# A hybrid decoder layer on one core: the last layer norm without GpSimd arithmetic, its bias written ahead and added to by transfers

## The chip, the core and the metric

The kernel runs on one core of a Trainium2 chip. A core has a matrix engine (TensorE, in the profile PE, its weight loads PEld), three engines for elementwise work (VectorE = DVE, ScalarE = ACT, GpSimd = POOL), an engine that here only issues transfers (SyncE = SP), and 16 DMA engines that move data between the memory of the chip (DRAM) and the core's own memory (SBUF). Matrix products land in PSUM, eight banks of 128 x 512 f32. The metric is the time of one execution in microseconds on the device: the median over several runs.

## The reference, cut to what matters

One decoder layer on 1024 tokens of 1024 channels: a token mixer (convolution, state-space model, attention), a first layer norm, and a mixture of experts with a shared expert, then a second layer norm. All is f32. The change is in the second norm and its inputs:

```
y = routed_experts(h2d, e_idx, e_w, ...) + swiglu(h2d, shared ...)
x = layer_norm(DEEPNORM_ALPHA * x + g2 * y, ln_g[l, 1], ln_b[l, 1])

def layer_norm(x, g, b):            # over the 1024 channels of a token
    mu = mean(x); var = mean(square(x - mu))
    return (x - mu) * rsqrt(var + 1e-5) * g + b
```

Each token goes to two experts, so the routed part of y is a sum of two rows.

## The kernel before, in words

The stages stand in `build` one after the other: `mixer` (with `front`, the state-space parameters on POOL, and the projections), `attention`, `merge` (output weights of the attention branch, gates), `ffn` (first norm, routing, shared expert), `experts` (blocks of 128 rows, one after the other, inside conditional stretches), `final`.

`experts` writes each result row, already weighted, by an indirect transfer on POOL's queue (line 1672) into a DRAM array `yd` of 2 x 1024 rows: first choices, then second choices. The shared expert's part and the residual are already summed in eight SBUF tiles `base[i]`, 128 tokens x 1024 channels each.

`final` works through the same eight tiles of 128 tokens. First it loads the gate g2, the gain and the bias of the norm as three rows of 4 KB on SP (line 1714), spreads each over 128 partitions by TensorE products with a row of ones (line 1719), and ACT copies the result to SBUF (line 1720). Sixteen loads of 512 KB on SP bring both rows of each token (line 1729); they wait for the last indirect transfer of the experts. Then, for a tile:

- `gated`: the two rows are added and multiplied by g2. For tiles 0 and 1 (`DG`) DVE does both on 128 x 1024 (lines 1735 and 1736). For the others TensorE adds them, with the identity as the weights (line 1741), and DVE multiplies out of PSUM in two halves (line 1742).
- `total`: DVE adds `base` and sums over channels in one instruction (line 1746), ACT makes the negative mean (1751) and the sum of squares (1753).
- `root`, `norm`: ACT makes variance and root (1759, 1760), DVE refines the reciprocal by three instructions on 128 x 1 (1763 to 1765).
- For tiles 0 to 4, ACT applies mean and scale (1775), and `affine` lets POOL multiply by the gain and add the bias (1781, two instructions on 128 x 1024). For tiles 5 to 7 (`LAST = 5`) DVE does it in two instructions (1798, 1783).
- SP stores the tile (line 1784).

Outside the stretches marked `manual_schedule` (parts of the front, the router and the experts), a planner orders the instructions of every engine before the kernel runs. It takes them by their place in the program, but one that has nothing to wait for can be put ahead of earlier ones that have. On the chip each engine and each of its queues goes through its instructions in that order.

Of the kernel before, what the change touches and what calls it, by code (L numbers as in the profile page):

```python
# [10 lines left out]
F32 = mybir.dt.float32  # L11
# [3 lines left out]
AF = mybir.ActivationFunctionType  # L15
ALU = mybir.AluOpType
# [4 lines left out]
D = 1024  # L21
S = 1024
NT = S // 128
# [20 lines left out]
LN_EPS = 1e-5  # L44
# [23 lines left out]
LT = 5  # L68
LGI, DV, DG = 2, (6, 7), (0, 1)
# [11 lines left out]
class K:  # L81
# [86 lines left out]
    def build(self):  # L168
        with ExitStack() as ctx:
# [24 lines left out]
                self.attention()  # L194
            if self.stop == "att":
                return
            self.mgp = pool(est, "mgp")
            self.mh, self.ml = ([self.part(z, c) for c in range(4)] for z in "hl")
            self.wof = pool(est, "wof")
# [1506 lines left out]
    def final(self, P):  # L1706

        nc = self.nc
        v, act, gp, pe = nc.vector, nc.scalar, nc.gpsimd, nc.tensor
        ys = []  # L1710

        row = P.tile([128, 3, D], F32, name="frow")
        for i, src in enumerate((self.adad[3:4, :], self.a["ln_g"][1:2, :], self.a["ln_b"][1:2, :])):
            nc.sync.dma_start(out=row[0:1, i], in_=src)
        g2, lg, lb = (P.tile([128, D], F32, name=n) for n in ("g2", "lg2", "lb2"))
        for i, t in enumerate((g2, lg, lb)):
            for n in range(2):
                ps, sl = self.ps("y"), slice(n * 512, (n + 1) * 512)
                pe.matmul(ps[:], self.ones[0:1, :], row[0:1, i, sl], start=True, stop=True)
                act.copy(out=t[:, sl], in_=ps[:])  # L1720
        st = P.tile([128, 6, NT], F32, name="fst")
        eps = P.tile([128, 1], F32, name="feps")
        v.memset(eps[:], LN_EPS)

        act.activation(out=st[:, 5, 0:1], in_=self.ones[:, 0:1], func=AF.Sqrt)
        for i in range(NT):
            ys.append([P.tile([128, D], F32, name=f"fy{k}", tag=f"fy{k}", bufs=NT) for k in range(2)])
            for k in range(2):
                nc.sync.dma_start(out=ys[i][k][:], in_=self.yd[k * S + i * 128:k * S + (i + 1) * 128, :])
        c = lambda n, i: st[:, n, i:i + 1]  # L1730

        def gated(i, n):
            if i in DG:
                if n == 0:
                    v.tensor_tensor(out=ys[i][0][:], in0=ys[i][0][:], in1=ys[i][1][:], op=ALU.add)
                    v.tensor_tensor(out=ys[i][0][:], in0=ys[i][0][:], in1=g2[:], op=ALU.mult)
                return
            sl = slice(n * 512, (n + 1) * 512)
            ps = self.ps("y")
            for k in range(2):  # L1740
                pe.matmul(ps[:], self.ident[:], ys[i][k][:, sl], start=k == 0, stop=k == 1)
            v.tensor_tensor(out=ys[i][0][:, sl], in0=ps[:], in1=g2[:, sl], op=ALU.mult)

        def total(i):
            r = ys[i][0]
            v.scalar_tensor_tensor(out=r[:], in0=r[:], scalar=1.0, in1=self.base[i][:], op0=ALU.mult, op1=ALU.add,
                                   accum_out=c(0, i))
            if i in DV:
                v.tensor_scalar(out=c(2, i), in0=c(0, i), scalar1=-1.0 / D, scalar2=None, op0=ALU.mult)
            else:  # L1750
                act.mul(out=c(2, i), in_=c(0, i), mul=-1.0 / D)
            junk = P.tile([128, D], BF, name="junk", tag="junk", bufs=2)
            act.activation(out=junk[:], in_=r[:], func=AF.Square, bias=c(2, i), accum_out=c(3, i))

        def root(i):
            if i in DV:
                v.tensor_scalar(out=c(3, i), in0=c(3, i), scalar1=1.0 / D, scalar2=LN_EPS, op0=ALU.mult, op1=ALU.add)
            else:
                act.activation(out=c(3, i), in_=c(3, i), func=AF.Identity, scale=1.0 / D, bias=eps[:])
            act.activation(out=c(4, i), in_=c(3, i), func=AF.Sqrt)  # L1760

        def norm(i):
            v.reciprocal(out=c(4, i), in_=c(4, i))
            v.scalar_tensor_tensor(out=c(5, i), in0=c(4, i), scalar=c(3, i), in1=c(4, i), op0=ALU.mult, op1=ALU.mult)
            v.tensor_scalar(out=c(5, i), in0=c(5, i), scalar1=-0.5, scalar2=1.5, op0=ALU.mult, op1=ALU.add)
            if i in DV:
                v.tensor_tensor(out=c(4, i), in0=c(4, i), in1=c(5, i), op=ALU.mult)
            else:
                act.activation(out=c(4, i), in_=c(4, i), func=AF.Identity, scale=c(5, i))
            if i < LAST:  # L1770
                if i in DV:
                    v.tensor_tensor(out=c(2, i), in0=c(2, i), in1=c(4, i), op=ALU.mult)
                else:
                    act.activation(out=c(2, i), in_=c(2, i), func=AF.Identity, scale=c(4, i))
                act.activation(out=ys[i][0][:], in_=ys[i][0][:], func=AF.Identity, scale=c(4, i), bias=c(2, i))

        def affine(i):
            r = ys[i][0]
            if i < LAST:
                for e, row, op in zip(GL[i], (lg, lb), (ALU.mult, ALU.add)):  # L1780
                    (v if e == "v" else gp).tensor_tensor(out=r[:], in0=r[:], in1=row[:], op=op)
            else:
                v.scalar_tensor_tensor(out=r[:], in0=ys[i][1][:], scalar=c(4, i), in1=lb[:], op0=ALU.mult, op1=ALU.add)
            nc.sync.dma_start(out=self.out[i * 128:(i + 1) * 128, :], in_=r[:])

        GL = ('gg', 'gg', 'gg', 'gg', 'gg', 'vv', 'vv', 'vv')
        LAST = LT
        with ExitStack():
            for j in range(NT + 2):
                if j < NT:  # L1790
                    gated(j, 0)
                    gated(j, 1)
                if 0 < j < NT:
                    root(j - 1)
                if j < NT:
                    total(j)
                    if j >= LAST:
                        v.scalar_tensor_tensor(out=ys[j][1][:], in0=ys[j][0][:], scalar=c(2, j), in1=lg[:], op0=ALU.add, op1=ALU.mult)
                    if j == NT - 1:
                        norm(j - 1)  # L1800
                        affine(j - 1)
                        affine(j - 2)
                        root(j)
                        norm(j)
                        affine(j)
                        break
                if j:
                    norm(j - 1)
                if j > 1:
                    affine(j - 2)  # L1810


class Route:
# [290 lines left out]
```

## Time and profile before

| | us |
|---|---|
| median of 3 runs | 1587.35 (1585.13 to 1588.13) |
| the profiled execution, its own time | 1582.0 |
| its span | 1579.9 |
| PE busy | 1419.6 (90%) |
| DVE busy | 1196.8 (76%) |
| ACT busy | 733.4 (46%) |
| POOL busy | 442.5 (28%) |

The span runs from the first to the last record of the profile; the execution's own time is 2.1 us longer. Mean granted TensorE clock: 0.954 of full speed. Times in the rows below are microseconds from the span's start unless they are marked ns.

### The profile page before, as it was taken

What the parts mean: (1) busy time and instruction counts of PE and PEld (TensorE: products, weight loads), DVE (VectorE), ACT (ScalarE), POOL (GpSimd) and SP (SyncE); (2) the same over time, 40 slices, a digit from 0 to 9 for tenths busy, and PEclk for the clock granted to TensorE, in tenths of its full rate; (3) what the DMA queues carried; (4) which work ended last, traced back from release to release, by engine and by line L of the source; (5) the groups of instructions that cost most, each with busy time, mean ns of one, the idle gap of its engine ahead of it and who ended that gap; (6) DMA issues with size and microseconds to landing.
All of it is one profiled execution on the core that took longest, in us unless ns stands there. A gap on an engine that the chain in (4) does not pass through costs nothing.

```text
span 1579.9 us, 20183 instructions
## 1 busy us (share of the span) xinstructions
PE 1419.6 (90%) x6996; PEld 1144.4 (72%) x6996; DVE 1196.8 (76%) x1861; ACT 733.4 (46%) x1192; POOL 442.5 (28%) x599
## 2 busy tenths in 40 slices
PE   5599799479999999999799979999979999999983
PEld 3477678368888887887588867788967888888841
DVE  8464687898775547756587788778887999999948
ACT  6232112242223334130477763335424998999853
POOL 7999930000000000006211252400322322222216
PEclk9799999799999999999799998999999999999977
DMA  9232221132122248968200035634623777777643
GB/s 382 80 113 88 73 58 27 67 101 97 56 107 107 107 145 308 326 161 224 36 15 12 4 114 192 225 133 151 251 79 115 303 282 287 289 297 272 255 182 146
DMA packets 79940, 247.50 MB, mean 157 GB/s; under 512 B 18460, under 2 KB 29780, under 8 KB 71000
## 3 DMA queue, kind: packets, MB, share of 16 engines
q1 hardware_dynamic: 53670, 200.47, 36.0%
q10 hardware_dynamic: 15218, 24.68, 4.5%
q0 software_dynamic: 10944, 20.99, 4.2%
q8 instruction: 56, 0.92, 0.2%
q14 instruction: 52, 0.43, 0.1%
HBM read 252.74 MB, written 55.10 MB: 195 GB/s over the span
## 4 chain that ended last, share of the span: by engine, by line
PE 58%; DVE 14%; POOL 12%; DMA 7%; issue 5%; ACT 3%; ACTq 0%; DVEq 0%; POOLq 0%; SPq 0%
PE ps_mm L140 9%; PE ps_mm L141 9%; PE ps_mm L142 9%; DMA yd<-y,idx 4%; PE ps_up L140 3%; PE ps_h L140 3%; PE ps_h L142 3%; PE ps_h L141 3%; PE ps_up L141 3%; PE ps_up L142 3%; PE ps_O L1272 2%; PE ps_T L1258 2%; PE ps_y L140 1%; PE ps_y L142 1%; PE ps_tr L1635 1%
## 5 line engine op out<-in xcount | busy, mean ns | idle before, releaser
L1138 POOL TENSOR_TENSOR mg<-mg,sg 128x512 f32<-128x512 f32 x16 | 23.5, 1476 | 496.4 <-DVE sg L1137 492.8
L140 PE MATMUL ps_mm<-hh,wlo 128*128 128x512 f32 x304 | 123.5, 406 | 22.7 <-ACT sg L1075 15.6
L142 PE MATMUL ps_mm<-hh,whi 128*128 128x512 f32 x304 | 123.1, 405 | 0.0
L141 PE MATMUL ps_mm<-hl,whi 128*128 128x512 f32 x304 | 122.7, 404 | 0.0
L125 ACT CAST whi<-raw 128x1024 fp32r<-128x1024 f32 (+1 forms) x45 | 46.8, 1040 | 134.0 <-PE ps_up L142 65.2
L1672 POOL DMA_INDIRECT yd<-y,idx x33 | 46.5, 1409 | 170.4 <-ACT y L1671 98.4
L140 PEld LDWEIGHTS ps_mm<-hh,wlo 128*128 128x128 f32 x304 | 58.7, 193 | 37.6 <-ACT sg L1075 16.1
L129 DVE TENSOR_TENSOR qh<-wo,qh 128x1024 fp32r<-128x1024 f32 x66 | 80.5, 1220 | 5.1 <-ACT qh L125 5.1
L129 DVE TENSOR_TENSOR ql<-wo,ql 128x1024 fp32r<-128x1024 f32 x66 | 79.5, 1219 | 4.8 <-ACT ql L125 4.8
L129 DVE TENSOR_TENSOR wlo<-raw,whi 128x1024 fp32r<-128x1024 f32 x44 | 60.4, 1373 | 26.5 <-ACT whi L125 26.5
L125 ACT CAST qh<-wo 128x1024 fp32r<-128x1024 f32 x66 | 70.0, 1061 | 4.1 <-DMA wo<-exp 4.1
L142 PEld LDWEIGHTS ps_mm<-hh,whi 128*128 128x128 f32 x304 | 58.6, 193 | 14.9 <-issue 1.0
L141 PEld LDWEIGHTS ps_mm<-hl,whi 128*128 128x128 f32 x304 | 58.8, 193 | 13.7 <-issue 0.2
L125 ACT CAST ql<-wo 128x1024 fp32r<-128x1024 f32 x66 | 68.2, 1052 | 0.0
L125 ACT CAST xh<-ps_tr 128x512 fp32r<-128x512 f32 x66 | 39.5, 599 | 55.5 <-PE ps_tr L1635 55.4
L1610 POOL DMA_INDIRECT xg<-h2d,idx x35 | 37.1, 1061 | 77.1 <-PE ps_tr L1635 63.5
L1244 DVE TENSOR_REDUCE sm<-ps_S 128x1 f32<-128x256 f32 (+3 forms) x64 | 49.2, 770 | 10.8 <-PE ps_S L1241 10.1
L129 DVE TENSOR_TENSOR pl<-ps_T,ph 128x512 fp32r<-128x512 f32 (+1 forms) x80 | 45.9, 581 | 14.0 <-ACT ph L125 12.6
L140 PE MATMUL ps_up<-ah,wlo 128*128 128x512 f32 x128 | 50.6, 403 | 5.1 <-ACT ah L125 2.9
L391 DVE TENSOR_TENSOR sp<-ps_mm,sp 128x512 f32<-128x512 f32 x48 | 32.8, 686 | 28.0 <-PE ps_mm L142 27.8
L1245 ACT ACTIVATE p<-ps_S,sm 128x256 f32<-128x256 f32 (+3 forms) x64 | 48.5, 758 | 10.0 <-DVE sm L1244 9.4
L140 PE MATMUL ps_mm<-wo,ml 128*128 128x512 f32 x128 | 50.0, 398 | 2.8 <-DVE sg L1354 2.8
(727 smaller groups left out, 4733.2 us busy)
## 6 DMA issues: line engine op xcount, KB each, us to landing
wo<-exp SPq DMA_DIRECT2D x111, 1024.0 KB
raw<-w_in SPq DMA_DIRECT2D x43, 512.0 KB
adr<-w_ada SPq DMA_DIRECT2D x32, 512.0 KB
wada<-w_ada SPq DMA_DIRECT2D x16, 512.0 KB
fy<-yd SPq DMA_DIRECT2D x16, 512.0 KB
sga<-sg ACTq DMA_DIRECT2D x8, 512.0 KB
sgc<-sg ACTq DMA_DIRECT2D x8, 512.0 KB
sgs<-sg ACTq DMA_DIRECT2D x8, 512.0 KB
```

The lines of the kernel that those rows point to most:

```text
L125: nc.scalar.copy(out=hi, in_=src)
L129: e.tensor_tensor(out=lo, in0=src, in1=hi.bitcast(F32), op=ALU.subtract)
L140: mm(ps, wl, xh, start=first, stop=False)
L141: mm(ps, wh, xl, start=False, stop=False)
L142: mm(ps, wh, xh, start=False, stop=last)
L391: v.tensor_tensor(out=out, in0=p, in1=x, op=op)
L1244: v.tensor_reduce(out=sm[:], in_=x, axis=AX.XY if two else AX.X, op=ALU.max, negate=True)
L1245: act.activation(out=y, in_=x, func=AF.Exp, bias=sm[:], accum_out=d)
L1258: pe.transpose(pt[:, k2 * 256 + qi * 128:k2 * 256 + qi * 128 + 128], prob[h, c, qi][:, ks], self.ident[:])
L1272: pe.matmul(po[:, 0:256], vv[:, kt, h].rearrange("p z d -> p (z d)"), x[z], start=kt == 0 and z == 0, stop=kt == 2 * c + 1 and z == 1)
L1610: self.nc.gpsimd.indirect_dma_start(out=self.xg[b % 2][:], out_offset=None, in_=self.h2d[:], in_offset=bass.IndirectOffsetOnAxis(ap=self.i ...
L1672: nc.gpsimd.indirect_dma_start(out=self.yd[:], in_=y[:], in_offset=None, out_offset=bass.IndirectOffsetOnAxis(ap=self.idx[:, 1, b:b + 1], ...
```

## The change

In `build`, right behind the attention and ahead of the merge, SP gets one more transfer: the bias row is written to all 1024 rows of the output (4 MB, DRAM to DRAM). In `final`, the bias is gone from the arithmetic: every tile is finished in SBUF without it, and POOL issues a transfer that adds the tile to what stands in the output. TensorE adds the experts' rows of all eight tiles. POOL computes nothing. The gate and the gain come spread over 128 partitions by two transfers on ACT's queue; the rows, the products with ones and the copies are gone. All tiles have one form and one order.

```diff
@@ build, behind self.attention()
+            self.nc.sync.dma_start(out=self.out[:, :], in_=self.a["ln_b"][1:2, :].partition_broadcast(S))
@@ final
-        row = P.tile([128, 3, D], F32, name="frow")
-        for i, src in enumerate((self.adad[3:4, :], self.a["ln_g"][1:2, :], self.a["ln_b"][1:2, :])):
-            nc.sync.dma_start(out=row[0:1, i], in_=src)
-        g2, lg, lb = (...)            # each: 2 x (pe.matmul(ones, row) -> PSUM, act.copy -> SBUF)
+        g2, lg = (P.tile([128, D], F32, name=n) for n in ("g2", "lg2"))
+        nc.scalar.dma_start(out=g2[:], in_=self.adad[3:4, :].partition_broadcast(128))
+        nc.scalar.dma_start(out=lg[:], in_=self.a["ln_g"][1:2, :].partition_broadcast(128))
...
         def total(i):
             r = ys[i][0]
+            for n in range(2):
+                sl = slice(n * 512, (n + 1) * 512)
+                ps = self.ps("y")
+                for k in range(2):
+                    pe.matmul(ps[:], self.ident[:], ys[i][k][:, sl], start=k == 0, stop=k == 1)
+                v.tensor_tensor(out=r[:, sl], in0=ps[:], in1=g2[:, sl], op=ALU.mult)
             v.scalar_tensor_tensor(out=r[:], in0=r[:], scalar=1.0, in1=self.base[i][:], ..., accum_out=c(0, i))
+            act.mul(out=c(2, i), in_=c(0, i), mul=-1.0 / D)
             act.activation(out=junk[:], in_=r[:], func=AF.Square, bias=c(2, i), accum_out=c(3, i))
+            act.activation(out=c(3, i), in_=c(3, i), func=AF.Identity, scale=1.0 / D, bias=eps[:])
             act.activation(out=c(4, i), in_=c(3, i), func=AF.Sqrt)

         def norm(i):
+            q = ys[i][1]
+            v.scalar_tensor_tensor(out=q[:], in0=ys[i][0][:], scalar=c(2, i), in1=lg[:], op0=ALU.add, op1=ALU.mult)
             v.reciprocal(out=c(4, i), in_=c(4, i))
             ...                       # the same two 128 x 1 instructions on DVE
+            act.activation(out=c(4, i), in_=c(4, i), func=AF.Identity, scale=c(5, i))
+            act.activation(out=q[:], in_=q[:], func=AF.Identity, scale=c(4, i))
+            gp.dma_start(out=self.out[i * 128:(i + 1) * 128, :], in_=q[:], accum_op=ALU.add)
+
+        for i in range(NT + 1):
+            if i < NT:
+                total(i)
+            if i:
+                norm(i - 1)
```

`gated`, `root`, `affine` with its POOL instructions, the stores on SP, and the loop with its special cases for the last tiles are removed.

## Rows read from the trace of the kernel before

**Rows 1.** Chain of waits, its end: start us, length us, what.
```profile
1522.44 4.39 DMA fy<-yd
...
1526.93 1.23 DVE fy L1735
...
1574.62 1.28 DVE fy L1783
```

**Rows 2.** DVE groups, 1522 to 1580: line engine operation tiles shapes xcount | busy us, mean ns | idle.
```profile
L1746 DVE SCALAR_TENSOR_TENSOR fy<-fy,b 128x1024 f32<-128x1024 f32 x8 | 13.6, 1700 | 0.2
L1764 DVE SCALAR_TENSOR_TENSOR fst<-fst 128x1 f32<-128x1 f32 x8 | 9.7, 1208 | 0.1
L1742 DVE TENSOR_TENSOR fy<-ps_y,g 128x512 f32<-128x512 f32 x12 | 7.9, 682 | 0.0
L1798 DVE SCALAR_TENSOR_TENSOR fy<-fy,fst,lg 128x1024 f32<-128x1024 f32 x3 | 4.8, 1603 | 0.0
...
L1765 DVE TENSOR_SCALAR fst<-fst 128x1 f32<-128x1 f32 x8 | 1.2, 150 | 0.2
```

**Rows 3.** Timeline of the last norm, DVE and POOL: start, length, instruction [idle before <-releaser].
```profile
1529.52 1.23 DVE L1746 SCALAR_TENSOR_TENSOR fy<-fy,b 128x1024 f32<-128x1024 f32 x1
...
1536.81 0.22 DVE L1764 SCALAR_TENSOR_TENSOR fst<-fst 128x1 f32<-128x1 f32 x1
...
1537.84 5.67 POOL L1781 TENSOR_TENSOR fy<-fy,lg 128x1024 f32<-128x1024 f32 x2 [20.15 <-DVE fy L1742]
...
1538.56 2.72 DVE L1746 SCALAR_TENSOR_TENSOR fy<-fy,b 128x1024 f32<-128x1024 f32 x1
```

**Rows 4.** Timeline of the last norm, TensorE.
```profile
1520.42 10.57 PE L1719 MATMUL ps_y<-frow,ones 1*128 1x512 f32 x12 [4.71 <-DMA frow<-adad]
...
1531.85 23.11 PE L1741 MATMUL ps_y<-fy,ident 128*128 128x512 f32 x48 [0.86 <-DMA fy<-yd]
```

**Rows 5.** Windows: stretch, PE PEld DVE ACT POOL busy, granted clock, DMA share, GB/s.
```profile
80.00:84.00 4.00, 4.00 (x14) 3.15 (x13) 1.52 (x2) 1.39 (x2) 4.00 (x16) 0.71 0.00 0
...
1536.00:1538.00 2.00, 2.00 (x5) 0.83 (x4) 1.32 (x5) 1.97 (x7) 0.16 (x1) 0.90 1.02 406
...
1542.00:1544.00 2.00, 2.00 (x6) 0.88 (x5) 1.10 (x3) 1.30 (x4) 2.00 (x2) 1.00 0.97 387
```

**Rows 6.** ACT groups, 1515 to 1580.
```profile
L1753 ACT ACTIVATE junk<-fy,fst 128x1024 bf16<-128x1024 f32 x8 | 9.2, 1148 | 5.5 <-DVE fst L1749 5.3
L1775 ACT ACTIVATE fy<-fy,fst 128x1024 f32<-128x1024 f32 x5 | 6.2, 1241 | 0.1
L1769 ACT ACTIVATE fst<-fst 128x1 f32<-128x1 f32 x6 | 1.7, 287 | 3.5 <-DVE fst L1765 3.5
```

**Rows 7.** The mixer's 512 KB stores on POOL's queue: issue min/median/max ns; time to landing.
```profile
L1140 POOL DMA_DIRECT2D mgd<-mg x8: 556/568/797, 723.9 to 754.8; - x8
...
DMA to landing us min/median/max: 3.7/7.2/13.1
```

**Rows 8.** Windows of half a microsecond at the end of the span.
```profile
1577.50:1578.00 0.50, 0.00 (x0) 0.00 (x0) 0.00 (x0) 0.00 (x0) 0.00 (x0) 0.50 0.99 410
1578.00:1578.50 0.50, 0.00 (x0) 0.00 (x0) 0.00 (x0) 0.00 (x0) 0.00 (x0) 0.50 0.06 17
```

**Rows 9.** Timelines of the front: SP, ACT, PE.
```profile
19.39 2.85 SPq L118 DMA_DIRECT2D raw<-w_in  x3
...
75.75 0.78 ACT L579 ACTIVATE ht<-ps_x,col 128x512 f32<-128x512 f32 x1 [24.47 <-DMA csd<-sn]
...
76.58 1.12 PE L570 MATMUL ps_x<-ident,x 128*128 128x128 f32 x4 [18.20 <-ACT ht L579]
```

**Rows 10.** Attention: a window with a spread row, an idle one; ACT at its end.
```profile
868.00:869.00 1.00, 0.92 (x8) 0.91 (x8) 0.66 (x3) 0.93 (x4) 0.00 (x0) 1.00 1.04 254
...
885.00:895.00 10.00, 9.96 (x67) 8.30 (x66) 7.86 (x15) 7.77 (x21) 0.00 (x0) 1.00 0.00 0
...
937.84 1.05 ACT L125 CAST whi<-raw 128x1024 fp32r<-128x1024 f32 x1 [2.37 <-DMA raw<-w_up_attn]
```

More of the change, by code (lines that the diff above doesn't have):

```diff
@@ L1709, in final @@
         v, act, gp, pe = nc.vector, nc.scalar, nc.gpsimd, nc.tensor
-        ys = []
-        row = P.tile([128, 3, D], F32, name="frow")
-        for i, src in enumerate((self.adad[3:4, :], self.a["ln_g"][1:2, :], self.a["ln_b"][1:2, :])):
-            nc.sync.dma_start(out=row[0:1, i], in_=src)
[L1715 to L1720, printed above, removed]
+        g2, lg = (P.tile([128, D], F32, name=n) for n in ("g2", "lg2"))
+        nc.scalar.dma_start(out=g2[:], in_=self.adad[3:4, :].partition_broadcast(128))
+        nc.scalar.dma_start(out=lg[:], in_=self.a["ln_g"][1:2, :].partition_broadcast(128))
         st = P.tile([128, 6, NT], F32, name="fst")
@@ L1725, in final @@
         act.activation(out=st[:, 5, 0:1], in_=self.ones[:, 0:1], func=AF.Sqrt)
+        ys = [[P.tile([128, D], F32, name=f"fy{k}", tag=f"fy{k}", bufs=NT) for k in range(2)] for i in range(NT)]
         for i in range(NT):
-            ys.append([P.tile([128, D], F32, name=f"fy{k}", tag=f"fy{k}", bufs=NT) for k in range(2)])
             for k in range(2):
@@ L1730, in final @@
         c = lambda n, i: st[:, n, i:i + 1]
[L1732 to L1742, printed above, removed]
         def total(i):
             r = ys[i][0]
+            for n in range(2):
[4 more added lines that the diff above has]
+                v.tensor_tensor(out=r[:, sl], in0=ps[:], in1=g2[:, sl], op=ALU.mult)
             v.scalar_tensor_tensor(out=r[:], in0=r[:], scalar=1.0, in1=self.base[i][:], op0=ALU.mult, op1=ALU.add,
                                    accum_out=c(0, i))
[L1748 to L1751, printed above, removed]
+            act.mul(out=c(2, i), in_=c(0, i), mul=-1.0 / D)
             junk = P.tile([128, D], BF, name="junk", tag="junk", bufs=2)
             act.activation(out=junk[:], in_=r[:], func=AF.Square, bias=c(2, i), accum_out=c(3, i))
[L1755 to L1759, printed above, removed]
+            act.activation(out=c(3, i), in_=c(3, i), func=AF.Identity, scale=1.0 / D, bias=eps[:])
             act.activation(out=c(4, i), in_=c(3, i), func=AF.Sqrt)
         def norm(i):
+            q = ys[i][1]
+            v.scalar_tensor_tensor(out=q[:], in0=ys[i][0][:], scalar=c(2, i), in1=lg[:], op0=ALU.add, op1=ALU.mult)
             v.reciprocal(out=c(4, i), in_=c(4, i))
@@ L1765, in norm @@
             v.tensor_scalar(out=c(5, i), in0=c(5, i), scalar1=-0.5, scalar2=1.5, op0=ALU.mult, op1=ALU.add)
[L1766 to L1810, printed above, removed]
+            act.activation(out=c(4, i), in_=c(4, i), func=AF.Identity, scale=c(5, i))
```

## The prediction, made before the changed kernel ran

> **What bounds the kernel now.** Read the chain of waits from its end: it names the stage where time can be won. Its last 57 us are the last norm. The first pair of row loads lands at 1526.8 (1522.44 + 4.39), and from 1526.93 to 1574.62 + 1.28 = 1575.9 DVE is on the chain nearly without a break [rows 1]. So DVE bounds this stage: 49.0 us for eight tiles.
>
> Then the groups of DVE, to see what it does in that time. The sum over the tile (L1746) has a mean of 1700 ns and the smallest of instructions, 128 x 1 (L1764), a mean of 1208 ns [rows 2]. The timeline says why: alone, the same two take 1.23 and 0.22 us; the sum that starts at 1538.56 takes 2.72 us while POOL multiplies two SBUF tiles from 1537.84 on [rows 3]. DVE instructions with two SBUF operands are held up by POOL's. Against 1.21, 0.22 and 1.28 us undisturbed, the three lines lose 13.6 - 8 x 1.21 = 3.9, 9.7 - 8 x 0.22 = 7.9 and 4.8 - 3 x 1.28 = 1.0 us [rows 2, 3]: 12.8 us that are no work of DVE's.
>
> After DVE's end the last store goes. The windows show its data moving at 410 GB/s until shortly after 1578.0 [rows 8]; the span ends at 1579.9. The tail behind the last instruction is 4.0 us.
>
> TensorE works at half clock when the stage begins: twelve products of one row fill 1520.4 to 1531.0 [rows 4], the full ones start at 1531.85, and the granted clock is 0.90 in 1536 to 1538 and then 1.00 [rows 5]: full at about 1536.3, 4.4 us after their start. The front has another such rise: work begins at 76.58 after a pause of 18.2 us [rows 9], and 80 to 84 has a mean of 0.71 [rows 5], so the rise is near 82.3, 5.8 us after.
>
> **The change, part by part.**
>
> *POOL's arithmetic goes.* The 12.8 us of hold-ups go with it. DVE's own work in a tile becomes: two halves out of PSUM 2 x 0.68, sum with its readout 1.24, (x - mean) x gain 1.28 (L1798 undisturbed), three small instructions 0.53 together: 4.41 us, of which 2.60 in `total` and 1.81 in `norm` [rows 2, 3]. Eight tiles: 35.3 us against 49.0.
>
> *TensorE adds all rows.* It loses the cover that DVE's sums of tiles 0 and 1 gave it while the clock was low. A tile is 8 instructions. In the 23.11 us of its 48 [rows 4], 4.4 at half clock, one takes 20.9 / 48 = 0.435 us at 2.4 GHz and 0.87 at 1.2. It can start with the first 512 KB block, at about 1525.7 (half a pair earlier; the pairs follow at (1544 - 1526.9) / 7 = 2.4 us, the loads being over in the window 1542 to 1544 [rows 1, 5]). The two ACT-queue loads of gate and gain move 1 MB ahead of and beside the first blocks; they can be issued as the experts end, when the old rows were loaded, some 1.5 us ahead of the first product's 1520.42 [rows 4], and the row loads begin at 1522.44, so I charge 0.4 us of the 2.6 us that 1 MB takes at 400 GB/s; ends 0 and 2.6 [rows 1, 5]. Start 1526.1, half clock for 5.2 us (between the two rises): 6 instructions, so tile 0 is summed at 1531.3 + 2 x 0.435 = 1532.2, tile 1 at 1535.7, then one each 3.5 us, the last at 1556.6. The clock costs nothing more, since from tile 2 on 3.5 us are less than DVE's 4.41.
>
> *DVE.* Total of tile 0 is over at 1532.2 + 0.68 + 1.24 = 1534.1, of tile 1 at 1537.6. Should the planner put norm 0 into the gap ahead of tile 1, up to 1.3 us are won; I take the order of the program. Left are eight norms (14.5) and six totals (15.6): DVE ends at 1567.7, the last total at 1564.1.
>
> *ACT.* Per tile 1.15 + 0.19 for the squares, 1.24 for the scaling and four small ones of 0.2 to 0.29 [rows 6]: 3.6 us, under DVE's 4.41. At the end it becomes late: root of tile 7 at 1564.1 + 2.1 = 1566.2, scale of tile 6 until 1567.75, then tile 7's factor (0.29) and scaling (1.24): 1569.3. That is the new last instruction, 6.6 us ahead of the old.
>
> *The transfer that adds.* The trace has none. It has POOL's 512 KB stores, each taking the queue 0.57 us and landing 3.7 us (shortest), 7.2 (median), 13.1 (longest) after issue [rows 7]; nothing else of POOL's waits behind it now. What lies in the output has to be read too, 512 KB more: 1.3 us at 410 GB/s [rows 8]. Bounds for the tail: 4.0 us, as SP's store has now (the same bytes and one read more exclude a shorter one), and 0.3 + 13.1 + 1.3 + 0.9 = 15.6 by the longest landing. I take 0.3 wait + 3.7 + 1.3 + 0.9 from landing to the end of the span (of the 4.0 now I count 3.1 as issue and landing) = 6.2, because nothing else uses the DMA engines then: 2.2 more than now. The seven before it go beside DVE's work.
>
> The Trainium skill, "Collectives: The Full Stack", section on the bandwidth ceiling, says that a reducing transfer is slower by its two source reads and not by the addition, at half a copy's rate. By it one transfer would hold the engines for 2.6 us and eight for 21 us, spread over the 28 us from tile 0's end to the last: no queue, and the same tail. No run shown here has such a transfer.
>
> *The bias into the output.* 4.2 MB DRAM to DRAM have no row. At the 410 GB/s of the last store that is 10 us [rows 8]; at the 254 GB/s of a window in which one row is spread over many and the engines are full, 17 [rows 10]. It waits for nothing, so the planner may move it ahead of the attention, as it moved loads of `w_in` into the front's SP queue at 19.39, ahead of transfers that come earlier in the program [rows 9]. Inside the attention the DMA engines are idle (share 0.00 in 885 to 895) [rows 10]: price 0. In the front it delays the loads behind it, but there PE later idles 18.2 us and ACT 24.5 us, waiting for POOL's parameters [rows 9]: 10 to 17 us fit, price 0; above 18 the excess would count. I take 0; the bad place is a rival.
>
> *Removed rows, products, copies, bias instructions:* off the path or inside the DVE sum.
>
> **Sum.** Last instruction -6.6, tail +2.2: -4.4 us. The profiled execution's own time, 1582.0 (2.1 us around its span of 1579.9), becomes 1577.6; that execution lies 0.34% under the median of the runs shown, and scaled to the median 1587.35 it is 1582.9 us.
>
> **The rivals.**
>
> *The adding transfers become the bound.* Place: POOL's queue from about 1541.3 (tile 0 scaled). Eight at X us each end at 1541.3 + 8X + 4; that exceeds the old 1579.9 from X = 4.3 on. For it: the median landing of 7.2 and the longest of 13.1 [rows 7]. Against it: those shared the engines with loads, and a landing time is not an occupancy. At X = 5.5 it ends at 1589.3, 9.4 us later than before: 1597 us. Chance 0.12.
>
> *The bias goes right ahead of the merge's weights*, at its place in the program. At 937.84 ACT has already waited 2.37 us for the first of them [rows 10]; ACT and DVE stand still with the rest of the attention queued behind. 10 to 17 us come on the path, less 4.4: 1593 to 1600. Against it: the planner moves what is free to go. Chance 0.09.
>
> *The tail eats the gain.* The last transfer lands after the median of 7.2 plus the second read: tail 9.7, which is 5.7 more than now and 6.6 earlier: gain 0.9; or the clock rises 2 us later and the loads of gate and gain cost 2.6. Within 3 us of before: 1585.5. Chance 0.22.
>
> *Something elsewhere is re-ordered*, since a new SP instruction shifts the planner's times: slower by 4 to 8 us, chance 0.05.
>
> *It does not do what it says:* the bias may run in the front and not in the attention; by the above without a price, inside the forecast.
>
> **How the numbers follow.** The forecast has 0.52; its own range is 1579 (norm 0 in the gap, tail 4.0) to 1584. About 0.2%, 3.2 us, is what a measurement of this kernel can tell. Faster by more: 0.52, the forecast's. Same: 0.22, the tail. Slower: 0.12 + 0.09 + 0.05 = 0.26. The range 1578.5 to 1595 takes in the longest tail (15.6: 5.0 slower than before, 1592); it leaves out a few hundredths below, and above it half or more of the two slow rivals.
>
> **What would show it.** DVE's L1746 and L1764 successors at 1.2 and 0.22 us in all eight tiles; no POOL arithmetic after 1520; TensorE's sums starting near 1526 at half clock, full by 1532; DVE gapless from tile 2; last ACT scaling 6 to 7 us earlier than the old last DVE instruction; 6 us from there to the end. It is wrong if the adding transfers stand back to back after the last scaling, if DVE keeps waiting for PSUM after tile 2, or if the difference is already there before the experts begin.

## The result, and the profile after

| | before | after |
|---|---|---|
| median of 7 runs each, us | 1585.5 (1582.2 to 1588.1) | 1594.1 (1588.4 to 1600.8) |
| profiled execution, own time | 1582.0 | 1593.1 |
| its span | 1579.9 | 1591.0 |
| last indirect store of the experts issued (L1672, after L1674) | 1516.7 | 1529.1 |
| from there to the end of the span | 63.2 | 61.9 |

The change makes the kernel slower: ratio 1.0053, 95% interval 1.0033 to 1.0074, some 8.6 us. Forecast were 1582.9 us, 0.52 for faster. The last two rows of the table say where to look: the last norm is 1.3 us shorter, and everything ahead of it 12.4 us longer. The difference is there before the experts begin, which the prediction named as a sign of its being wrong.

The last norm first. DVE's groups in 1530 to 1591 of the kernel after (line numbers are 2 higher than before up to the last norm, whose lines are new):

```profile
L1734 DVE TENSOR_TENSOR fy<-ps_y,g 128x512 f32<-128x512 f32 x16 | 10.6, 680 | 11.8 <-PE ps_y L1733 11.8
L1745 DVE SCALAR_TENSOR_TENSOR fy<-fy,fst,lg 128x1024 f32<-128x1024 f32 x8 | 10.2, 1274 | 0.3 <-ACT fst L1737 0.3
L1735 DVE SCALAR_TENSOR_TENSOR fy<-fy,b 128x1024 f32<-128x1024 f32 x8 | 9.7, 1219 | 0.1
L1747 DVE SCALAR_TENSOR_TENSOR fst<-fst 128x1 f32<-128x1 f32 x8 | 1.7, 213 | 0.0
```

This is as forecast: against [rows 2], the sum has a mean of 1219 ns in place of 1700, and the smallest instruction 213 in place of 1208. POOL's hold-ups are gone, and once TensorE delivers (11.8 us idle) DVE has hardly a pause. TensorE starts 9.4 us after the experts' last indirect store, as forecast (1526.1 - 1516.7), at half clock, and is at full clock some 3.5 us later (0.54 in 1541 to 1542, 1.00 in 1542 to 1543). Its timeline, and then windows (the granted clock is the third column from the end; [rows 4, 5] are the old ones):

```profile
1538.44 22.14 PE L1733 MATMUL ps_y<-fy,ident 128*128 128x512 f32 x47 [10.39 <-DMA fy<-yd]
```

```profile
1538.00:1542.00 4.00, 3.56 (x5) 1.54 (x6) 0.00 (x0) 0.00 (x0) 0.00 (x0) 0.51 0.96 335
...
1574.00:1578.00 4.00, 0.00 (x0) 0.00 (x0) 0.72 (x5) 3.97 (x8) 1.72 (x2) 0.50 0.90 136
1578.00:1582.00 4.00, 0.00 (x0) 0.00 (x0) 0.00 (x0) 0.12 (x1) 0.86 (x1) 0.50 1.02 186
1582.00:1586.00 4.00, 0.00 (x0) 0.00 (x0) 0.00 (x0) 0.00 (x0) 0.00 (x0) 0.50 0.92 181
1586.00:1591.00 5.00, 0.00 (x0) 0.00 (x0) 0.00 (x0) 0.00 (x0) 0.00 (x0) 0.50 0.01 1
```

Read the end here: no engine computes after 1578.1, but the DMA engines (share in the last column but one) are full until about 1586 at 181 to 186 GB/s, where the old last store moved its data at 410 [rows 8]; then 5 us pass in which nothing moves. The last adding transfer is issued at 1578.4, 12.6 us ahead of the end; the old last store was 4.0 us ahead.

Now the write of the bias. One row of SP's queue, and three windows:

```profile
24.10 0.67 SPq L198 DMA_DIRECT2D out<-ln_b  x1
```

```profile
36.00:40.00 4.00, 3.99 (x20) 2.93 (x19) 1.95 (x4) 2.50 (x3) 3.65 (x7) 0.92 0.97 175
40.00:44.00 4.00, 3.27 (x15) 2.31 (x13) 0.00 (x0) 0.00 (x0) 3.71 (x7) 1.00 0.98 210
44.00:48.00 4.00, 0.00 (x0) 0.00 (x0) 0.00 (x0) 0.00 (x0) 3.60 (x12) 0.86 1.03 206
```

It runs in the front and not in the attention. The DMA engines are full at a low rate, 147 to 217 GB/s, from 34 to 50 us; 4.2 MB at 206 to 210 GB/s would take some 20 us. From there the two traces part. The same events of both (after minus before):

| event | offset, us |
|---|---|
| last load of the front's weights issued (L506) | +18.9 |
| first copy of the state-space input (L866) | +5.7 |
| last load of the state-space input back (L1005, 204 us) | -2.1 |
| last row of the state-space output stored (L1054, 243 us) | +4.5 |
| first product of the pair projections taken by DVE (L391, 339 us) | +11.9 |
| last indirect store of the experts (L1672) | +12.4 |

All is lost before 340 us. But what the front loses is won back by 204 us, and the loss that stays arises between there and 340.

### The profile page after: what moved, and what is told of

It is laid out like the page before. It is cut to its first block, busy times and chain, and to the rows that moved or that the text cites. A ratio compares the mean times of both kernels' runs of the same rounds, so it can differ in the third digit from the quotient of the medians.

```text
span 1591.0 us, 20181 instructions
## 1 busy us (share of the span) xinstructions
PE 1420.8 (89%) x7000; PEld 1145.5 (72%) x7000; DVE 1181.4 (74%) x1857; ACT 732.2 (46%) x1190; POOL 418.1 (26%) x597
## 4 chain that ended last, share of the span: by engine, by line
PE 41%; DMA 19%; POOL 14%; DVE 11%; issue 11%; ACT 2%; ACTq 0%; POOLq 0%; SPq 0%; DVEq 0%
DMA yd<-y,idx 11%; PE ps_mm L140 9%; PE ps_mm L141 9%; PE ps_mm L142 9%; PE ps_O L1274 2%; DMA adr<-w_ada 2%; PE ps_T L1260 2%; DMA xg<-h2d,idx 1%; PE ps_S L140 1%; PE ps_S L142 1%; PE ps_S L141 1%; PE ps_up L140 1%; DMA sg<-sgs 1%; PE ps_up L142 1%; PE ps_up L141 1%
## 5 line engine op out<-in xcount | busy, mean ns | idle before, releaser
L140 PEld LDWEIGHTS ps_mm<-hh,wlo 128*128 128x128 f32 x304 | 59.9, 197 | 46.1 <-ACT sg L1077 15.9
L1674 POOL DMA_INDIRECT yd<-y,idx x33 | 47.3, 1433 | 169.4 <-ACT y L1673 103.3
```

Source lines behind the costliest of these rows:

```text
L140: mm(ps, wl, xh, start=first, stop=False)
L1674: nc.gpsimd.indirect_dma_start(out=self.yd[:], in_=y[:], in_offset=None, out_offset=bass.IndirectOffsetOnAxis(ap=self.idx[:, 1, b:b + 1], ...
```

## The experiments

Ratios are to the kernel before on the same chip, with their 95% intervals; 1.0020 is about 3.2 us. Beside them the kernel before had medians of 1584.6 us (e1 to e4), 1583.9 (e5 to e8 and e12 to e14) and 1582.5 (e9 to e11). What a run gains or loses is given below as the difference of medians; by the ratios they come out up to 2.5 us larger or smaller.

| run | median, us | ratio |
|---|---|---|
| e1_bias_alone | 1592.2 | 1.0062 (1.0041 to 1.0083) |
| e2_bias_eighth | 1584.6 | 1.0006 (0.9994 to 1.0019) |
| e3_bias_late | 1585.1 | 1.0004 (0.9987 to 1.0021) |
| e4_norm_nobias | 1580.6 | 0.9979 (0.9964 to 0.9994) |
| e5_bias_half | 1593.7 | 1.0064 (1.0049 to 1.0078) |
| e6_bias_double | 1589.7 | 1.0050 (1.0031 to 1.0068) |
| e7_hybrid6 | 1577.5 | 0.9966 (0.9951 to 0.9980) |
| e8_norm_sp | 1571.6 | 0.9931 (0.9913 to 0.9949) |
| e9_write_pinned | 1593.7 | 1.0072 (1.0056 to 1.0088) |
| e10_before_pinned | 1583.0 | 1.0004 (0.9991 to 1.0017) |
| e11_hybrid5_pinned | 1573.2 | 0.9925 (0.9908 to 0.9942) |
| e12_cast_behind | 1589.4 | 1.0043 (1.0025 to 1.0060) |
| e13_casts_behind | 1591.8 | 1.0055 (1.0036 to 1.0074) |
| e14_norm_dve_bias | 1582.7 | 0.9997 (0.9980 to 1.0014) |

### The write or the norm?

```diff
 e1: the kernel before, behind self.attention():
+            self.nc.sync.dma_start(out=self.out[:, :], in_=self.a["ln_b"][1:2, :].partition_broadcast(S))
 e2: the same for out[0:128, :]
 e3: the kernel after; in divide(3) of the attention the last load is kept as self.anchor, and
+            with self.tc.issue_after(self.anchor):
                 self.nc.sync.dma_start(out=self.out[:, :], ...)
 e4: the kernel after without the write, and
-            gp.dma_start(out=self.out[...], in_=q[:], accum_op=ALU.add)
+            gp.dma_start(out=self.out[...], in_=q[:])
```

> The kernel before plus the one transfer that writes the bias row to all 1024 rows of the output, at its place in the program behind the attention; the last norm is the old one and stores over it. Theory A (the loss is made by this transfer in the front, where the planner puts it): about 12 us slower than before, 1597 us, with the offset in the trace growing from 0 to 12 us between 50 and 340 us, and a last norm as long as before (63 us from the last indirect transfer's issue to the end of the span). Theory B (the adding transfers at the end cost the time, the write is free): within 3 us of before. Theory C (both in parts): between 4 and 8 us slower.

> As the run above, but the added transfer writes 128 rows only (0.5 MB instead of 4.2), and the old norm stores over it. The order of the instructions on the engines then stays the old one until the merge, where it changes in the same way. Theory A: 0.5 MB take some 2.5 us of the DMA engines, which the cover of 18 us in the front swallows: within 2 us of before, 1584 to 1588. Rival (any extra transfer upsets the planner's order in the merge and the experts, and this is what costs): as slow as the full write, or slower than before by more than 4 us.

> The kernel after, its bias write bound behind a small load in the middle of the attention on SP's queue, where the DMA engines are nearly idle; all else as changed. Theory A: the 12 us in the front go, and only the last norm's own difference is left (1.3 us shorter from the last indirect transfer's issue to the end): 1582 to 1587. Theory B: still 6 to 10 us slower than before, 1592 to 1596. Rival C: the write delays the merge's weights by 3 to 8 us: 1588 to 1592, with the loss between 930 and 960 us in the trace.

> The changed last norm without the bias write, and with plain stores on POOL's queue in place of the adding transfers; the last norm's bias is left out. The front and all stages up to the last norm keep the old order. Theory A with costly adding transfers at the end (they queue and hold the DMA engines at 100 to 200 GB/s until 5 us before the end): DVE's 6 to 7 us come through, 1577 to 1580. Rival (the loads of gate, gain and rows, and the clock's rise at the start of the norm, eat the gain): the same as before, 1583 to 1587.

The write alone costs 7.6 us, nearly the whole loss (e1; theory A had 12, and by its size this is theory C's 4 to 8), and bound into the attention it costs none (e3; issued at 866.3, and the offset at 340 us is -1.0). An eighth of it costs nothing (e2). The new norm with all its parts but the bias gains 4.0 us (e4), and with the adding transfers and a late write it gains nothing (e3). So theory A held for the place, and both of its expectations for the norm were near. e2 seemed to say that bytes make the difference; the next pair shows that they don't.

### Bytes, or the order that the planner makes?

```diff
 e5: the kernel before +  out[0:512, :] written with the bias
 e6: the kernel before +  the full write, twice
```

> The kernel before plus a write of the bias to 512 rows of the output (2.1 MB, half of the full write), stored over by the old norm. PE, DVE, POOL and SP then have their instructions in exactly the order of the run with the full write. Theory bytes (the front can hide some 18 to 20 us of transfer, and only what exceeds it costs): 2.1 MB take 10 us, the state-space input's first copy is not later than before by more than 1 us, and the time is within 2 us of before, 1583 to 1587. Theory order (the planner's new order of front and projections costs, whatever the bytes): as slow as the full write, 1590 to 1594.

> The kernel before plus the full bias write issued twice (8.4 MB), stored over by the old norm. Theory bytes: the second write of 20 us lies wholly beyond the cover, so 18 to 22 us more than the one full write, 1610 to 1615. Theory order, or another wait than the ada loads behind it that sets the front's end: less than 8 us more than one write, 1592 to 1600.

Theory bytes fell on both sides. Half of the write is as slow as the whole, and twice the write is not slower (e6 came out below both of its ranges). In their traces e1 and the kernel after have the same order on all engines up to the last norm, and e5 and e6 have it but for single rows. Against before, some 220 rows of TensorE stand elsewhere, all between 100 and 250 us, and fewer rows of the others. With e2 the old order stays, in the merge too, but for the write itself and one row of ACT. So it is the new order of the engines' instructions that costs; not one of the rows that move is a line of the change.

### Which part of the new order?

The first place that the traces show is in the front. ACT issues four small transfers of rotary tables (csd, L791), which wait for POOL until 70 to 76 us; the planner puts them among ACT's work on eight channel blocks. Before they have two blocks behind them, in e5 three, in e1 four, and the first copy of the state-space input comes at 88.5, 92.9 and 95.1. e9 and e10 bind the four behind all blocks; in both, nothing else changes its place.

```diff
 e9 = e1, e10 = the kernel before, both with
+            with self.tc.issue_after(self.last_ht):
                 nc.scalar.dma_start(out=dst.rearrange("f (b t) -> (f b) t", b=8), in_=src)
```

> The kernel before plus the full bias write in the front (the first run's kernel), with one thing changed: ACT's four issues of the rotary tables (csd), which wait for POOL until about 72 us and which the planner put behind channel block 3 of the front, in the midst of the blocks, are bound behind ACT's last instruction of the front's blocks. All other engines keep the order of the first run's kernel. Theory place (the write costs because the planner, seeing the loads later, puts ACT's waiting issues ahead of two more blocks): the first copy of the state-space input comes at 75 to 80 us in place of 95.1, the front's loss of 6.6 us goes, and the time is 1583 to 1588. Rival bytes (the loads held up by 20 us of transfer set the front's end): that copy still at 93 or later and 1590 to 1594.

> The control: the kernel before, no bias write, with the same four issues bound behind the front's last block on ACT; nothing else changes its order. The first copy of the state-space input then comes at 66 to 72 us in place of 88.5. If POOL's parameters set the end of the stage that follows (POOL is busy for 105 of 110 us in 90 to 200), the time is as before within 3 us; if the state-space input is what the stage waits for, it is 5 to 12 us faster, 1572 to 1579.

The first copy of the state-space input (ACT's timeline, e9 and then e10):

```profile
82.84 1.07 ACT L869 COPY uq<-ps_mm 128x512 f32<-128x512 f32 x2 [5.00 <-PE ps_mm L598]
```

```profile
78.18 1.07 ACT L867 COPY uq<-ps_mm 128x512 f32<-128x512 f32 x2 [15.01 <-POOL nr L825]
```

It is 12.3 and 10.3 us earlier than in e1 and before, and the time is the same in both pairs. The delay in the front, the only one that the prediction had priced, is free. The stretch behind it seems to wait for POOL, which is busy for 105 of the 110 us in 90 to 200. Theory place fell as well; the control e10 says why.

That left 200 to 340 us. ACT's timeline there, weight conversions (whi) and copies of the state-space output (Y) alone, before, after, and in e12:

```profile
229.22 1.07 ACT L1051 COPY Y<-ps_ss 128x512 f32<-128x512 f32 x2 [11.27 <-PE ps_ss L1046]
232.66 1.05 ACT L125 CAST whi<-raw 128x1024 fp32r<-128x1024 f32 x1 [2.37 <-PE ps_mm L142]
238.22 1.07 ACT L1051 COPY Y<-ps_ss 128x512 f32<-128x512 f32 x2 [4.51 <-PE ps_ss L1046]
```

```profile
230.18 1.08 ACT L1053 COPY Y<-ps_ss 128x512 f32<-128x512 f32 x2 [13.43 <-PE ps_ss L1048]
242.75 1.07 ACT L1053 COPY Y<-ps_ss 128x512 f32<-128x512 f32 x2 [11.49 <-PE ps_ss L1048]
243.71 1.06 ACT L125 CAST whi<-raw 128x1024 fp32r<-128x1024 f32 x1
```

```profile
225.50 1.07 ACT L1054 COPY Y<-ps_ss 128x512 f32<-128x512 f32 x2 [9.89 <-PE ps_ss L1049]
238.81 1.07 ACT L1054 COPY Y<-ps_ss 128x512 f32<-128x512 f32 x2 [12.24 <-PE ps_ss L1049]
239.77 1.06 ACT L125 CAST whi<-raw 128x1024 fp32r<-128x1024 f32 x1
```

Before, the conversion of the last query projection's weights stands between the two pairs of copies; after, behind both. ACT is idle for 11.5 us ahead of the second pair, but it goes through its queue in order. What hangs on it is seen on DVE and PE (before, after, e12):

```profile
233.74 1.23 DVE L129 TENSOR_TENSOR wlo<-raw,whi 128x1024 fp32r<-128x1024 f32 x1
...
235.61 1.28 DVE L907 COPY cq<-ps_mm 128x512 f32<-128x512 f32 x2
...
237.43 0.71 PE L1046 MATMUL ps_ss<-s,G 64*128 64x128 f32 x8
238.07 0.50 PE L140 MATMUL ps_mm<-hh,wlo 128*128 128x512 f32 x1
```

```profile
244.80 1.23 DVE L129 TENSOR_TENSOR wlo<-raw,whi 128x1024 fp32r<-128x1024 f32 x1 [10.94 <-ACT whi L125]
...
246.67 1.28 DVE L909 COPY cq<-ps_mm 128x512 f32<-128x512 f32 x2
...
247.41 0.79 PE L140 MATMUL ps_mm<-hh,wlo 128*128 128x512 f32 x1 [4.31 <-DVE cq L909]
```

```profile
240.86 1.22 DVE L129 TENSOR_TENSOR wlo<-raw,whi 128x1024 fp32r<-128x1024 f32 x1 [9.46 <-ACT whi L125]
...
242.73 1.28 DVE L910 COPY cq<-ps_mm 128x512 f32<-128x512 f32 x2
...
237.95 0.78 PE L1049 MATMUL ps_ss<-s,G 64*128 64x128 f32 x8
243.47 0.80 PE L140 MATMUL ps_mm<-hh,wlo 128*128 128x512 f32 x1 [4.73 <-DVE cq L910]
```

DVE goes through its queue in order too. The low part of these weights (wlo) waits for the conversion; the copies of the first projection's result (cq) stand behind it; and the next run of products on TensorE waits for these copies. From the end of the last state-space product to this run 4.73 us pass in e12. It is the same 4.73 us in all seven runs with the conversion behind the copies (after, e1, e5, e6, e9, e12, e13; where the write is in the front, with a single product in between); in before and the other eight the run follows at once.

e12 moves this one row in the kernel before, without any write of the bias. Every other row of every engine keeps its place. e13 also binds the conversion for the first query projection behind ACT's eight issues for the last state-space matrix, which gives all three conversions the places of the new order. Rows of TensorE change with it: 44 in the trace, 33 of them in the attention near 790 us.

```diff
 e12: the kernel before; s5_run keeps its last copy as self.last_Y, and for the last of the three projections
+        with self.tc.issue_after(self.last_Y):
             wh, wl = self.split(raw)
 e13: as e12, and the first of the three behind self.last_kq
```

> The kernel before, no bias write; one instruction of ACT changes its place: the conversion of the last query projection's weights is bound behind the last pair of state-space output copies, where the order with the bias write has it. Every other row on every engine stays. Theory cast (a projection's weights late by one copy leave TensorE without work, and its clock falls): TensorE waits 4 us near 245, the first product of the pair projections comes 4 to 9 us later, the time is 1587 to 1592. Rival (the other changed rows make the loss, or nothing else waits for this cast): within 2 us of before, 1581 to 1585.

> As the run above, with a second binding: the conversion for the first query projection stands behind the eight issues of the last state-space matrix on ACT, so that all three conversions have the places that the order with the bias write gives them; some 27 rows of TensorE change with it. Theory cast: most of the loss, 1590 to 1594. Rival: within 3 us of before.

Theory cast held in both. One conversion of 1.05 us costs 5.5 us (e12), against 5.8 to 11.2 us in the four runs of the kernel before with the write in the front. e13 has 7.9, but its interval overlaps that of e12, and with the other rows that it moves what the two further conversions cost is not told apart. The windows from 200 to 250 us (before, after, e12) show the size:

```profile
200.00:250.00 50.00, 47.39 (x292) 37.04 (x291) 36.51 (x61) 7.29 (x12) 10.14 (x16) 0.97 0.28 57
```

```profile
200.00:250.00 50.00, 42.05 (x257) 32.13 (x257) 31.12 (x53) 7.10 (x12) 7.81 (x16) 0.88 0.26 53
```

```profile
200.00:250.00 50.00, 41.60 (x249) 32.61 (x249) 35.07 (x60) 5.67 (x10) 8.27 (x12) 0.86 0.22 48
```

PE's busy time multiplied by its mean granted clock is 46.0, 37.0 and 35.8 us: 9 to 10 us of TensorE's work at full clock have moved out of this stretch. Where to, the products of the second and third projection show, 96 in number. In all three traces they stand in one run behind the last state-space product. Windows over that run (before, after, e12):

```profile
238.07:260.74 22.67, 22.67 (x99) 18.30 (x98) 14.76 (x22) 4.54 (x8) 0.00 (x0) 1.00 0.24 47
```

```profile
247.41:271.93 24.52, 24.52 (x97) 19.83 (x98) 15.52 (x23) 2.57 (x5) 0.00 (x0) 0.91 0.12 28
```

```profile
243.47:268.27 24.80, 24.80 (x97) 20.00 (x98) 15.61 (x23) 2.58 (x5) 0.00 (x0) 0.90 0.11 30
```

In e12 the run ends 7.5 us later than before: 4.7 are the wait, 2.1 the half clock at which TensorE starts after it, and 0.6 the state-space products' later end. In the kernel after it ends 11.2 us later: 4.7, 1.9, and 4.5 for the state-space products, whose last ends at 242.7 in place of 238.1. Which of the other moved rows makes these 4.5 us no run shows. The normalization and the pair projections wait for the last result of the three projections, copied out at 260.9 before (L907), at 272.0 after and at 268.3 in e12: their first product comes 11.9 us later after and 8.3 in e12. Not tried: the kernel after with the conversion put back between the copies.

### The tail of the norm

```diff
 e8: as e4, but the plain stores on SP:    nc.sync.dma_start(out=self.out[...], in_=q[:])
 e14: no write, no adding transfers; lb loaded as lg is, and in norm(i)
-            act.activation(out=q[:], in_=q[:], func=AF.Identity, scale=c(4, i))
+            v.scalar_tensor_tensor(out=q[:], in0=q[:], scalar=c(4, i), in1=lb[:], op0=ALU.mult, op1=ALU.add)
+            nc.sync.dma_start(out=self.out[...], in_=q[:])
 e7: as e3 with the write for 768 rows; tiles 6 and 7 as in e14, the others by adding transfers
 e11: the same with 640 rows and tiles 5 to 7, and the four issues bound as in e10
```

> The kernel after with the bias write bound into the middle of the attention, for 768 rows; tiles 0 to 5 go out by adding transfers as changed, tiles 6 and 7 get scale and bias from DVE in one instruction of 1.28 us and are stored by SP. In the run with the late write the last adding transfer was issued at 1564.8 and the span ended 12.2 us later; an SP store took 4.0 us. If the tail is what the adding transfers cost: DVE is 2.6 us longer, ACT's last scaling of 1.24 us goes, the tail is 4 to 5 us in place of 12.2, net 5 to 7 us less than the run with the late write: 1578 to 1580. Rival (the six adding transfers at 200 GB/s still hold the engines when the last two stores come, or DVE's longer tiles push everything back): 1583 to 1586.

> The changed norm without a bias write, with plain stores, as the run before it of that kind, but issued by SP and not by POOL; the last norm's bias is left out. There the last store was issued on POOL's queue at 1571.2 and the span ended 8.3 us later, against 4.0 us for SP's in the kernel before. If POOL's queue itself makes half of the long tail: 3 to 5 us less than with POOL's stores, 1576 to 1578. If the tail hangs on the data of the last two tiles only: the same, 1580 to 1581.

> The changed last norm without bias write and adding transfers: for all tiles DVE makes scale and bias in one instruction of 1.28 us in place of ACT's scaling, and SP stores. Against the run without a bias and with SP's stores (1571.6) DVE has eight instructions of 1.28 us more, 10.2 us, less 1.2 to 2.5 at the end where ACT's scaling stood: 1579 to 1581, a few us faster than before. Rival (TensorE or the row loads are late then, DVE has room for some of the eight): 1574 to 1577, as fast as the version with five adding tiles, which would make the adding transfers useless.

> Both together, as a version: tiles 0 to 4 by adding transfers, tiles 5 to 7 with scale and bias on DVE and SP's stores, the bias write of 640 rows bound into the middle of the attention, and the four issues of the rotary tables bound behind the front's blocks. Against the version with six adding tiles, DVE has 1.28 us more and one adding transfer of some 2.6 to 3.7 us less to wait for at the end: the norm within 1.5 us of that one's. With the front unchanged in time 1576 to 1579; with a faster front as the control shows it, less by that.

The stage alone, from the profiles:

| run | last store issued | to the end of the span | from the experts' last indirect store to the end |
|---|---|---|---|
| before: SP | 1575.9 | 4.0 | 63.2 |
| after: POOL, adding | 1578.4 | 12.6 | 61.9 |
| e3: POOL, adding | 1564.8 | 12.2 | 61.4 |
| e4: POOL, plain, no bias | 1571.2 | 8.3 | 58.1 |
| e8: SP, plain, no bias | 1565.1 | 4.0 | 53.5 |
| e14: SP, bias on DVE | | | 62.2 |
| e7: six adding, two on SP | | | 59.0 |
| e11: five adding, three on SP | | | 56.5 |

The windows of the end, e3, e4 and e8:

```profile
1566.00:1570.00 4.00, 0.00 (x0) 0.00 (x0) 0.00 (x0) 0.00 (x0) 0.00 (x0) 0.50 1.05 201
1570.00:1574.00 4.00, 0.00 (x0) 0.00 (x0) 0.00 (x0) 0.00 (x0) 0.00 (x0) 0.50 0.51 100
1574.00:1577.00 3.00, 0.00 (x0) 0.00 (x0) 0.00 (x0) 0.00 (x0) 0.00 (x0) 0.50 0.00 0
```

```profile
1570.00:1574.00 4.00, 0.00 (x0) 0.00 (x0) 0.00 (x0) 0.87 (x1) 0.86 (x2) 0.50 0.85 345
1574.00:1579.00 5.00, 0.00 (x0) 0.00 (x0) 0.00 (x0) 0.00 (x0) 0.00 (x0) 0.50 0.00 0
```

```profile
1566.00:1567.00 1.00, 0.00 (x0) 0.00 (x0) 0.00 (x0) 0.00 (x0) 0.00 (x0) 0.50 0.98 406
1567.00:1568.00 1.00, 0.00 (x0) 0.00 (x0) 0.00 (x0) 0.00 (x0) 0.00 (x0) 0.50 0.22 90
```

The tail has two prices of about 4 us each. With POOL's queue some 5 us pass between the last byte and the end of the span (e3: data until about 1572, end 1577.0; e4: 1574 and 1579.5); with SP's it is under 2 (e8: 1567.2 and 1569.1). That is e4 against e8, 8.3 against 4.0. And the adding transfers move half as many bytes in a second, so those of the last three tiles, issued at 1575.7 to 1578.4 in the kernel after, queue: e3 against e4, 12.2 against 8.3. The Trainium skill, "Collectives: The Full Stack", section on the bandwidth ceiling, gives a reducing transfer half of a copy's rate for its two source reads; it says so of a ring between cores. The rates here agree in size, 181 to 201 GB/s against 406 for the plain store. That the second read makes it is not shown: the plain write of the bias, DRAM to DRAM, was no faster (206 to 210).

e8 says how much the norm would gain if the bias were free: 9.7 us in the stage. Moving it to DVE gives that back (e14: eight instructions of 1.28 us; the time is the same as before, where 1579 to 1581 were expected). Some 2 us of that are not DVE's work: the bias then comes spread by a third transfer beside gate and gain, and DVE's first product stands 16.7 us behind the experts' last indirect store, against 14.3 in e8 (16.5 and 16.6 in e7 and e11). The transfers pay where their tail has time to drain: e7 and e11 use them for the first tiles, DVE and SP for the last ones, and are faster than both kernels. e11 has 0.9925, the best of all that compute everything; its binding of the four issues did nothing by itself (e10), and 6.7 us of its 9.3 are seen in the stage. e7 and e8 came out as expected or better, e11 3 us better than expected.

## Why the prediction was wrong, step by step

- *The bias into the output, price 0:* this step failed. It said that the planner may move the write into the front, and that there "10 to 17 us fit, price 0; above 18 the excess would count". The move was right, the transfer took some 17 to 20 us, and the delay that it made in the front is free (e9, e10). But the step priced the transfer's bytes alone, at the place where they move. With the write in the program the planner ordered rows of ACT, DVE, PE and POOL anew (why it chose so is not shown; that it reckons with later loads is likely). One of these rows, a conversion of 1.05 us put behind a wait, makes TensorE stand still for 4.7 us and go on at half clock; alone and without any write it costs 5.5 us (e12) of the 8.6. Where the rest comes from stays open. The rival "something elsewhere is re-ordered" was this, with 4 to 8 us and a chance of 0.05. The size was near and the chance was not: every write that was put in changed the order somewhere (e1, e2, e5, e6); the question is whether it hits a row that the path waits for.
- *POOL's arithmetic goes, DVE at 4.41 us a tile:* the hold-ups went as forecast, and the groups above and three smaller ones (1.2, 1.2, 0.6) sum to 35.2 us against 35.3. But a sum of lengths is not the time: DVE's records overlap by some 0.08 us from one to the next, and for the eight tiles the engine is busy for 31.2 us, 3.9 a tile (third figure behind the comma):

```profile
1543.00:1576.30 33.30, 24.88 (x58) 10.65 (x57) 31.20 (x64) 22.71 (x54) 5.07 (x6) 0.95 0.91 257
```

- *TensorE adds all rows, at half clock at first:* right: the start as forecast, the clock full after 3.5 us in place of 5.2, the end earlier than forecast. The last scaling was forecast 52.6 us after the experts' last indirect store (1569.3 - 1516.7); the transfer that follows it came at 49.3 (1578.4 - 1529.1). The 3.3 us fit DVE's shorter time, and the product of norm 0 stands in the gap ahead of tile 1, which the prediction had in its range alone.
- *Gate and gain cost 0.4 us:* inside that; not told apart.
- *The tail, 6.2 us:* mis-sized, 12.6 us within bounds of 4.0 to 15.6. The step took the shortest landing of POOL's stores because nothing else would use the engines. The other adding transfers do; and POOL's queue costs 4 us at the end with plain stores too. Of the 12.6 us some 8 pass until the last byte (forecast 5.3) and some 5 from there to the end (forecast 0.9).
- *The sum:* last instruction 3.3 us better, tail 6.4 us worse than forecast; the norm gains 1.3 us in place of 4.4. With the write kept out of the front the result is no change (e3), as the rival "the tail eats the gain" had it, at 1585.5. That the 1594.1 us measured lie in the range of 1578.5 to 1595 is luck: its upper end was worked out from the longest tail, not from a new order.
- *The adding transfers become the bound:* not from tile 0 on, as that rival put it; only for the last three.

## What to carry to other kernels

Where a planner orders the program, price an added instruction by the order that comes out, not by where its own work lies: build both orders and look for rows that wait in a queue and now have others behind them. A delay counts only if what follows waits for it; a control that takes the delay away in the old kernel (e10) tells this in one run. Transfers that add are cheap for early tiles and dear for the last: let them drain beside compute, and end on the queue with the shortest tail.

## What the runs showed that was not expected

- A 4.2 MB write from DRAM to DRAM held the DMA engines at 206 to 210 GB/s with a share of about 1.0, half of what a store from SBUF moved (406 to 410).
- POOL's issue of a 512 KB store takes 0.53 us (e4), of an adding one 0.86 us (after, e3), SP's 0.33 us (e8).
- The stretch from 200 to 340 us scatters by itself: with the same order of rows there, the first product of the pair projections came 1.0 us earlier (e3, e8) or 2.9 to 3.8 us later (e4, e2) than in the profile of before, and PE's busy time times clock in 200 to 250 was 46.1 (e3) or 41.8 us (e2). Part of it is the clock: the 96 products took 23.8 us in e2 and 23.3 in e4, at a mean of 0.95 and 0.97, against 22.7 at 1.00. Some 4 us of any two profiles' difference can come from there; the medians decide.
